# A decoder step on one core: operations of projection, samples and attention moved by a table of places, and the last norms, the tail and a first square root rearranged

## The chip, the cores and the metric

The kernel runs on one core of a Trainium2 chip. The metric is the device time of one execution in microseconds (us), the median of the runs. All engines run their own instructions in the order in which they were issued: TensorE (PE, with its weight loads as PEld), VectorE (DVE), ScalarE (ACT), GpSimd (POOL), and SP, which issues most of the transfers.

## The reference

One layer of a hybrid decoder for a prompt of 2048 rows and 8 samples of 4 rows, D = 1024, in float32:

```python
z = _rmsnorm(x, g) @ w_in                 # 1024 -> 2560: q, k, v (8 heads x 64), u, v (8 groups x 64)
for w, d in ((128, 1), (512, 4), (2048, 16)):
    s = q . k * 64**-0.5 + bias           # keys at distances 0, d, 2d, ..., w
    s = where(valid, s, NEG_INF)
    lse = logsumexp(s);  o = exp(s - lse) @ v
# the three branches are merged by position and head with weights from their softmax sums
# samples: the same with 4096 cached positions (a window of 2048 keys and values)
# the gating groups: u * (masked lower 128 x 128 W_s @ layernorm(v) + bias), in chunks of 128
x = x + concat(att, sgu) @ w_out          # output projection, 1024 x 1024
x = x + (silu(h @ w_gate) * (h @ w_up)) @ w_down    # h = _rmsnorm(x), width 2816
y = _rmsnorm(x)
```

`_rmsnorm(x, g)` is x * rsqrt(mean(x * x) + EPS) * g. Beside y, the last 2048 keys and values of prompt and samples and the normalised v rows of the samples are outputs.

## The kernel before

Every product is made in three passes: an operand is split into a high part (rounded for the fast form of float32 on PE) and a low part (the rest), and high x high, low x high and high x low are summed in PSUM. The high part is a copy on ACT, the low part a subtraction on DVE or POOL. So each weight goes through `w_load` (SP, line 231), `w_high` (ACT, line 236) and `w_low` (DVE, line 242).

The first 980 us are written as a plan. `Plan.at(step, phase, fn, *args)` notes an operation with a step, one of ten phases (early, exp, low, scores, turn, mid, values, out, misc, store) and a running number; `Plan.run` sorts by step, phase and number and calls them in that order. The order of the calls is the order of the instructions on each engine. The numbers count every call of `at` from the start of the program, so they name each operation. Steps up to 240 hold the input projection, the gating unit and the attention of the samples; from there on each of the eight heads has 20 steps.

Projection and samples. The weights run in as above; `transposed`, `value_split` (ACT, line 143, with pair as its result) and `store_values` (SP, line 379) put q, k and v into the buffers qk_d and v_d in memory; `gates`, `gated`, `gated_copy` (ACT, line 449) and `store_gated` (SP, line 452) do the gating unit, whose input v is normalised in `layer_norm_a` to `layer_norm_d` (lines 381 to 402) and split into vnh and vnl. The samples' scores are made on DVE: `key_unit` multiplies, `key_sum` (line 589) sums, `sample_bias` (lines 598 and 599) adds the bias; then `softmax_a` transposes and takes the maximum, `softmax_e` (ACT, lines 623 and 624) the exponential, `softmax_b` (DVE, lines 628 to 632) divides, `softmax_c` (PE, line 639) transposes back, and `value_high`, `value_low` (lines 663 and 667) and `value_unit` (PE, lines 678 and 679) multiply with the cached values.

Attention. A head is 16 tiles of 128 rows of the band (distances 1 and 4 together, up to five key tiles each, b0 to b15) and 4 strided steps (distance 16, four residues each, s0 to s3). A band tile goes through `band_scores` (PE, line 957), `band_bias` (DVE, line 963), `band_exp` (ACT, line 968), `band_turn` (PE transposes, line 976, and the high part ph on ACT, line 979), `low_parts` (DVE, line 998, pl), `band_values` (PE, line 1012) and `band_out`. A strided step goes through `order_queries` (POOL, line 941), `strided_scores` (PE, line 1030), `strided_bias` (DVE, lines 1035 and 1037, then a subtraction on POOL, line 1038), `strided_exp` (ACT, line 1041), `strided_sum` (DVE, line 1045), `strided_turn` (PE, line 1050; eh on ACT, line 1053; el on DVE, line 998) and `strided_values` (PE, lines 1061 and 1062). Band and strided transposes take the PSUM banks of one ring, and a bank comes free when its low part (pl or el) has been made.

At the end of a head `Stats` (POOL, line 1082, sm; PE, line 1088) and `Weights` (lines 1103 to 1135) make the factors of the branches, which are spread over the rows and written to f_d. One head later `merge_load` (SP, line 1149) brings four quarters of them back as pairs, and `merge` (POOL, lines 1160, 1162 and 1164) multiplies and adds. Meanwhile `load_head` loads the next head but one: q and k (line 901), the bias (line 906), the values for the strided steps in 8 transfers (line 917) and the values for the band in one of 1 MB (line 921). `roll` (line 173) copies a piece of the cache to the outputs.

From 980 us the rows are worked in blocks: output projection, the second norm (`norm2_half`, `norm2_gain`, `norm2_square`, `rms_b`, `norm2_scale`; lines 1497 to 1531), transposes (PE, line 1543), gate and up products (lines 1729 to 1731). At the end comes the down projection of the last rows (class `Down`): a step `n` sums and splits two operands (`split`: ACT lines 1926 and 1927, DVE lines 1928 and 1929), multiplies them for four row tiles (`mats`, lines 1943 to 1945) and adds to the rows (`evict`, line 1963). The final norm of a tile is `square` (ACT, line 1970), `mean` (DVE, lines 1990 and 1991), `root` (ACT, line 1994), `scale` (DVE, lines 150 to 154 and 2000), `scale_rest` (ACT, line 2004) and `out` (SP, line 2009). `behind(k, ...)` queues such a part k steps later. The last TAIL = 3 steps are done tile by tile, each tile with its own final norm behind it.

Of the kernel before, what the change touches and what calls it, by code (L numbers as in the profile page):

```python
# [19 lines left out]
P = 128  # L20
# [27 lines left out]

class Plan:
# [21 lines left out]
def hymba_step(ctx: ExitStack, tc: tile.TileContext, A: dict, O: dict):  # L71
# [1425 lines left out]
    def rms_b(s1, n, more=None):  # L1497
        if more is not None:
            dve.tensor_scalar(s1[:n, 0:1], s1[:n, 0:1], more[:n], None, op0=OP.add)
        dve.tensor_scalar(s1[:n, 1:2], s1[:n, 0:1], 1.0 / D, EPS, op0=OP.mult, op1=OP.add)  # L1500
        act.activation(s1[:n, 2:3], s1[:n, 1:2], AF.Sqrt)
# [6 lines left out]
    def norm2_half(B, i, junk=None):  # L1508

        B.s1[i] = s1 = fl.tile([P, 4], F32, name="s1", tag="s1", bufs=6)  # L1510
        act.activation(zn_tile() if junk is None else junk, B.acc[i][:, 0:512], AF.Square, accum_out=s1[:, 0:1])

    def norm2_gain(B, i):
        n = B.rows[i]
        B.xn[i] = square_tile() if n == P else fa.tile([P, D], F32, name="xns", tag="acc5")
        pool.tensor_mul(B.xn[i][:n], B.acc[i][:n], gain[0][:n])

    def norm2_square(B, i, junk):

        n = B.rows[i]  # L1520
        s1 = B.s1.get(i)
        if s1 is not None:
            act.activation(B.X[0][:, i, 0:512] if junk is None else junk, B.acc[i][:, 512:1024], AF.Square, accum_out=s1[:, 3:4])
            return s1, s1[:, 3:4]
        s1 = fl.tile([P, 4], F32, name="s1", tag="s1", bufs=6)
        act.activation(B.X[0][:, i, 0:D] if n == P else square_tile()[:n], B.acc[i][:n], AF.Square, accum_out=s1[:n, 0:1])
        return s1, None

    def norm2_scale(B, i, r):
        n = B.rows[i]  # L1530
        act.activation(B.xn[i][:n], B.xn[i][:n], AF.Copy, scale=r)
# [56 lines left out]
    def norm2_slot(B, k, order):  # L1588
# [278 lines left out]
    TAIL = 3  # L1867

    class Down:
# [97 lines left out]

        def square(self, i, c):
            x = self.acc[i][:, c * 512:(c + 1) * 512]
            act.activation(zn_tile(), x, AF.Square, accum_out=self.sq[i][:, (0, 3)[c == i % 2]:][:, 0:1])  # L1970

        def early_half(self, i):

            self.sq[i] = self.p2.tile([P, 4], F32, name="sq", tag="sq", bufs=8)
            c = i % 2
            x = self.acc[i][:, c * 512:(c + 1) * 512]
            self.behind(1, self.square, i, c)
            self.behind(1, pool.tensor_mul, x, x, gain[1][:, c * 512:(c + 1) * 512])

        def late_half(self, i, quick=False):  # L1980
            steps = (1, 2, 2, 3, 3, 4) if quick else (1, 2, 3, 4, 5, 6)
            for k, fn in zip(steps, (self.late_square, self.mean, self.root, self.scale, self.scale_rest, self.out)):
                self.behind(k, fn, i)
# [4 lines left out]
        def mean(self, i):  # L1988
            s1 = self.sq[i]
            dve.tensor_scalar(s1[:, 0:1], s1[:, 0:1], s1[:, 3:4], None, op0=OP.add)  # L1990
            dve.tensor_scalar(s1[:, 1:2], s1[:, 0:1], 1.0 / D, EPS, op0=OP.mult, op1=OP.add)

        def root(self, i):
            act.activation(self.sq[i][:, 2:3], self.sq[i][:, 1:2], AF.Sqrt)

        def scale(self, i):
            r = rms_c(self.sq[i], P)
            cs = slice((1 - i % 2) * 512, (2 - i % 2) * 512)
            x = self.acc[i][:, cs]
            dve.scalar_tensor_tensor(x, x, r, gain[1][:, cs], op0=OP.mult, op1=OP.mult)  # L2000

        def scale_rest(self, i):
            x = self.acc[i][:, i % 2 * 512:(i % 2 + 1) * 512]
            act.activation(x, x, AF.Copy, scale=self.sq[i][:, 2:3])
# [6 lines left out]
        def run(self):  # L2011
            self.queue = {}
            for n in range(2 * NS - TAIL):
# [13 lines left out]
                if n >= NJ and m < 4 and not (wide and j % 2):  # L2027
# [5 lines left out]
                    elif ps_ in (5, 6):  # L2033
                        self.late_half(i + ps_ - 5, not wide)
# [6 lines left out]
        def tail(self):  # L2041
            n0 = 2 * NS - TAIL
            for _ in range(4):
                tick()
            for n in sorted(self.queue):
                for fn, args in self.queue[n]:
                    fn(*args)

            def begin(m):
                i = 8 + 2 * m + 1  # L2050
                self.mean(i)
                self.root(i)

            def root_end(m):
                return rms_c(self.sq[8 + 2 * m + 1], P)

            def finish(m, r):
                i = 8 + 2 * m + 1
                x = self.acc[i]
                act.activation(x[:, 512:], x[:, 512:], AF.Copy, scale=r)  # L2060
                dve.scalar_tensor_tensor(x[:, 0:512], x[:, 0:512], r, gain[1][:, 0:512], op0=OP.mult, op1=OP.mult)
                self.out(i)

            r = {}
            for m in range(4):
                for n in range(n0, 2 * NS):
                    self.mats(n, (m,))
                if m:
                    begin(m - 1)
                    r[m - 1] = root_end(m - 1)  # L2070
                self.evict(1, 6, m, self.Y)
                self.late_square(8 + 2 * m + 1)
                if m:
                    finish(m - 1, r[m - 1])
            begin(3)
            finish(3, root_end(3))
# [156 lines left out]

    def first_block(B):
# [29 lines left out]

        def root_ahead():
            t_ = fl.tile([P, 4], F32, name="s1", tag="s1", bufs=6)
            act.activation(t_[:, 0:1], ident[:, 0:1], AF.Sqrt)
# [25 lines left out]
    def next_block(B, downs, finals):  # L2293
# [23 lines left out]
        for y in range(4):  # L2317
# [3 lines left out]
            else:  # L2321
                later(10 + 3 * y, sources, B, y // 2, y % 2 * 2, y % 2 * 2 + 1)
        for fn in downs:
# [201 lines left out]
```

## Time and profile before

| what | us |
|---|---|
| median of 3 runs | 2489.65 |
| the runs | 2488.77, 2489.65, 2495.33 |
| the profiled execution, its own time | 2492.2 |
| its span | 2490.4 |
| PE busy, share of the span | 2406.0, 97% |
| DVE, ACT and POOL busy | 1688.3, 1218.5, 1119.8 |
| mean granted TensorE clock | 0.988 |

Line numbers are those of the kernel before. A row of the timeline has start, duration, engine, line, operation, output and inputs, and in brackets the idle time before it with what ended that. A row of the waits has who waited for what, the total in us, how often, and the longest. A row of the windows has for each engine the busy time and the count of instructions, then the granted clock, the share of the transfer engines and GB/s.

### The profile page before, as it was taken

The page shows a single profiled execution, that of the slowest core. Times are in us where ns is not written, and L with a number is a line of the kernel's source. Part 1 is how long each engine was busy: PE and PEld are TensorE (multiplying, and loading weights), DVE is VectorE, ACT ScalarE, POOL GpSimd, SP SyncE. Part 2 cuts the span into 40 slices and gives each one's busy share as a digit, 9 for nine tenths or more (in the row PEclk, how much of TensorE's full clock was granted, in tenths as well). Part 3 has the DMA queues.
Part 4 walks back from the last instruction along what each step waited for, and adds up shares of the span by engine and source line. Part 5 has one row for each costly group of instructions (what it writes and reads, how often), then busy time and mean ns, then how long its engine had stood idle before and what let it go on. Part 6 is the DMA issues. An engine that isn't in the chain of part 4 may idle for free. (4 is left out here: it accounts for less than half of the span.)

```text
span 2490.4 us, 39073 instructions
## 1 busy us (share of the span) xinstructions
PE 2406.0 (97%) x13360; PEld 2128.3 (85%) x13360; DVE 1688.3 (68%) x3097; ACT 1218.5 (49%) x2414; POOL 1119.8 (45%) x859
## 2 busy tenths in 40 slices
PE   9999899999998889999999999999999999999997
PEld 6788667777888877999998899999799998888886
DVE  4378777335888786756655677766566666877886
ACT  6424344345777765433333533333465554445544
POOL 1004323013566666666664576667468883100100
PEclk9999999999999999999999999999999999999998
DMA  8863872688788856466668266676747677766842
GB/s 265 258 194 108 293 244 72 214 255 257 242 263 273 250 153 222 155 207 199 209 214 288 90 225 232 246 254 219 253 155 236 221 230 254 264 196 231 298 136 87
DMA packets 318087, 539.12 MB, mean 216 GB/s; under 512 B 28854, under 2 KB 152151, under 8 KB 312002
## 3 DMA queue, kind: packets, MB, share of 16 engines
q1 hardware_dynamic: 317536, 536.51, 65.8%
q8 instruction: 106, 1.74, 0.3%
q14 instruction: 91, 0.75, 0.1%
q10 hardware_dynamic: 354, 0.12, 0.0%
HBM read 420.38 MB, written 186.28 MB: 244 GB/s over the span
## 5 line engine op out<-in xcount | busy, mean ns | idle before, releaser
L1729 PE MATMUL ps_m<-xh,op 128*128 128x384 f32 (+5 forms) x1932 | 612.2, 317 | 0.3 <-DVE raw L1766 0.2
L1730 PE MATMUL ps_m<-xl,op 128*128 128x384 f32 (+5 forms) x1932 | 612.0, 317 | 0.0
L1731 PE MATMUL ps_m<-xh,op 128*128 128x384 f32 (+5 forms) x1932 | 611.3, 316 | 0.0
L1666 POOL TENSOR_TENSOR op<-fr,op 128x512 fp32r<-128x512 f32 x286 | 404.6, 1431 | 90.3 <-ACT op L1662 66.4
L1729 PEld LDWEIGHTS ps_m<-xh,op 128*128 128x128 f32 x1932 | 363.9, 188 | 1.6 <-DVE raw L1766 0.6
L1730 PEld LDWEIGHTS ps_m<-xl,op 128*128 128x128 f32 x1932 | 363.8, 188 | 0.6
L1731 PEld LDWEIGHTS ps_m<-xh,op 128*128 128x128 f32 x1932 | 364.2, 189 | 0.0
L1666 POOL TENSOR_TENSOR op<-pair,op 128x512 fp32r<-128x512 f32 x126 | 168.8, 1340 | 156.5 <-DVE hr L1791 86.1
L339 PE MATMUL ps_s<-wh,xh 128*128 128x512 f32 x480 | 197.8, 412 | 5.7 <-ACT xh L143 5.7
L1662 ACT ACTIVATE op<-fr 128x512 fp32r<-128x512 f32 x330 | 196.5, 621 | 10.0 <-DMA fr<-ab_d 6.2
L340 PE MATMUL ps_s<-wl,xh 128*128 128x512 f32 x480 | 190.7, 397 | 0.0
L341 PE MATMUL ps_s<-wh,xl 128*128 128x512 f32 x480 | 190.1, 396 | 0.0
L1780 ACT ACTIVATE ps_t<-zn 128x384 f32<-128x384 f32 (+2 forms) x132 | 60.0, 454 | 251.0 <-DVE zn L1759 205.7
L1926 ACT ACTIVATE op<-fr 128x512 fp32r<-128x512 f32 x140 | 88.7, 634 | 181.5 <-issue 87.7
L2036 POOL TENSOR_TENSOR ac<-ac,final_g 128x512 f32<-128x512 f32 x12 | 19.5, 1624 | 319.5 <-ACT zn L1970 311.2
L1928 DVE TENSOR_TENSOR op<-fr,op 128x512 fp32r<-128x512 f32 x140 | 102.2, 730 | 75.2 <-ACT op L1926 75.2
L1662 ACT ACTIVATE op<-pair 128x512 fp32r<-128x512 f32 x126 | 79.0, 627 | 109.9 <-DVE pair L1652 109.9
L339 PEld LDWEIGHTS ps_s<-wh,xh 128*128 128x128 f32 x480 | 92.2, 192 | 37.2 <-issue 10.3
L341 PEld LDWEIGHTS ps_s<-wh,xl 128*128 128x128 f32 x480 | 91.7, 191 | 20.6 <-DVE xl L146 0.2
L1943 PE MATMUL ps_m<-op 128*128 128x512 f32 x280 | 108.9, 389 | 0.0
L1944 PE MATMUL ps_m<-op 128*128 128x512 f32 x280 | 108.9, 389 | 0.0
L1945 PE MATMUL ps_m<-op 128*128 128x512 f32 x280 | 108.9, 389 | 0.0
(551 smaller groups left out, 5877.3 us busy)
## 6 DMA issues: line engine op xcount, KB each, us to landing
fr<-in_w_gate_dram SPq DMA_DIRECT2D x132, 256.0 KB
out_ks_dram<-in_cache_k_dram SPq DMA_DIRECT2D x56, 512.0 KB
out_vs_dram<-in_cache_v_dram SPq DMA_DIRECT2D x56, 512.0 KB
fr<-in_w_up_dram SPq DMA_DIRECT2D x110, 256.0 KB
fr<-ab_d SPq DMA_DIRECT2D x88, 256.0 KB
a<-h_d SPq DMA_DIRECT2D x80, 256.0 KB
fr<-t_d SPq DMA_DIRECT2D x80, 256.0 KB
raw<-in_w_in_dram SPq DMA_DIRECT2D x72, 256.0 KB
```

The source lines that it names most:

```text
L339: pe.matmul(o[j], xh[:, k, :], wh, start=(k == 0), stop=False)
L340: pe.matmul(o[j], xh[:, k, :], wl, start=False, stop=False)
L341: pe.matmul(o[j], xl[:, k, :], wh, start=False, stop=(k == KD - 1))
L1662: act.activation(ops[f, j][0], ab[f][j], AF.Copy)
L1666: (eng or pool).tensor_sub(lo_, ab[f][j], hi.bitcast(F32))
L1729: pe.matmul(out, wh[:, ks], xh[:, :, k], start=(k == 0), stop=False)
L1730: pe.matmul(out, wh[:, ks], xl[:, :, k], start=False, stop=False)
L1731: pe.matmul(out, wl[:, ks], xh[:, :, k], start=False, stop=(k == 3))
L1928: dve.tensor_sub(wl, w, wh.bitcast(F32))
L1943: pe.matmul(banks[m], hh[:, ts], wh, start=first, stop=False, skip_group_check=more)
L1944: pe.matmul(banks[m], hh[:, ts], wl, start=False, stop=False, skip_group_check=more)
L1945: pe.matmul(banks[m], hl[:, ts], wh, start=False, stop=j == NJ - 1, skip_group_check=more)
```

## The change

A table gives 282 of the planned operations another place, by steps and by phases. Its first lines, and how it is used:

```diff
+MOVES = {
+    0: (-1, 0), 1: (-1, 0), 2: (-1, 0), 59: (2, 0), 108: (-1, 0), 109: (-1, 0), 110: (-1, 0), 114: (2, 0),
+    115: (2, 0), 116: (2, 0), 144: (0, -2), 156: (-2, 0), 164: (0, -2), 177: (1, 0), 216: (-1, 0), 218: (1, 0),
...
     def at(self, step, phase, fn, *args):
-        self.events.append((step, self.PHASES.index(phase), self.n, fn, args))
+        steps, phases = MOVES.get(self.n, (0, 0))
+        place = max(0, min(len(self.PHASES) - 1, self.PHASES.index(phase) + phases))
+        self.events.append((step + steps, place, self.n, fn, args))
         self.n += 1
```

In the projection and the samples most moves are by one to three steps: numbers 108 to 110 and 114 to 116 are load, high and low part of the weights 44 and 46; many key sums come a step later; gates, their copies and stores 577 to 589 three steps later. In the heads the same moves come again and again: the band's second tile and its low parts by a phase, the strided sums two phases earlier, weights_e a step or a phase away, the loads of the next heads one to three steps later, one or two of the factor loads one or two steps away. In the changed kernel all line numbers of this part are 44 higher.

On SP, in the head from about 750 us, this is the stretch with the loads of the values (`v`, lines 917 and 921, 961 and 965 after) and of the factors of the head before (`pair`, line 1149, 1193 after); out_ks_dram is the roll. Before:

```order
L917 DMA v_7479<-v_d_67 16x16x128 x8
L173 DMA out_ks_dram<-in_cache_k_dram 16x8192
L921 DMA v_7542<-v_d_67 128x16x128
L1149 DMA pair_7564<-f_d_69 128x2x512
L1149 DMA pair_7566<-f_d_69 128x2x512
L173 DMA out_ks_dram<-in_cache_k_dram 16x8064
L1149 DMA pair_7729<-f_d_69 128x2x512
L173 DMA out_ks_dram<-in_cache_k_dram 16x8192
L901 DMA qh_7785<-qk_d_66 128x1x2048
```

And now:

```order
L961 DMA v_7479<-v_d_67 16x16x128 x8
L217 DMA out_ks_dram<-in_cache_k_dram 16x8192
L1193 DMA pair_7567<-f_d_69 128x2x512
L965 DMA v_7578<-v_d_67 128x16x128
L1193 DMA pair_7594<-f_d_69 128x2x512
L217 DMA out_ks_dram<-in_cache_k_dram 16x8064
L1193 DMA pair_7710<-f_d_69 128x2x512
L217 DMA out_ks_dram<-in_cache_k_dram 16x8192
L1193 DMA pair_7813<-f_d_69 128x2x512
```

The first of the pair loads stands ahead of the 1 MB load of v instead of behind it; the second and third stand one place further on.

On PE, in the same head, this is the stretch around the strided transposes (line 1050, 1094 after) of the last strided step, with those of the band (line 976, 1020 after), scores (line 957, 1001) and band products (line 1012, 1056). Before:

```order
L957 MATMUL ps_s_7761<-k_7268,qh_7238 128x256
L957 MATMUL ps_s_7761<-k_7268,ql_7295 128x256
L1050 MATMUL ps_t0_7764<-ident_80,e3_7681 128x128 x4
L976 MATMUL ps_t1_7772<-ident_80,e_7711 128x128 x4
L1012 MATMUL ps_o3_7731<-ph_7556,ve_6995 128x256
L1012 MATMUL ps_o3_7731<-pl_7557,ve_6995 128x256
```

And now:

```order
L1020 MATMUL ps_t0_7761<-ident_80,e_7725 128x128 x4
L1001 MATMUL ps_s_7767<-k_7293,qh_7241 128x256
L1001 MATMUL ps_s_7767<-k_7293,ql_7314 128x256
L1001 MATMUL ps_s_7770<-k_7293,qh_7241 128x384
L1001 MATMUL ps_s_7770<-k_7293,ql_7314 128x384
L1094 MATMUL ps_t1_7773<-ident_80,e3_7681 128x128 x4
L1056 MATMUL ps_o3_7733<-ph_7559,ve_7028 128x256
L1056 MATMUL ps_o3_7733<-pl_7560,ve_7028 128x256
```

The band's transposes of the tile e have moved from behind the strided ones of e3 to ahead of them, and the scores of a further tile (two rows with 384 columns) stand between.

On DVE, in the samples at about 280 us, this is the stretch from the maximum of a softmax (line 618, 662 after) to its division (lines 628 to 630, 672 to 674 after), with the low parts of weights wl (line 242, 286) and the samples' products and sums (lines 583 and 589, 627 and 633). Before:

```order
L618 TENSOR_SCALAR nm_2599<-nm_2599 128x1
L242 SCALAR_TENSOR_TENSOR wl_2603<-raw_2531,g1c_85,wh_2587 128x512
L589 TENSOR_REDUCE S_far_121<-pr_2553 128x8
L242 SCALAR_TENSOR_TENSOR wl_2625<-raw_2555,g1c_85,wh_2621 128x512
L589 TENSOR_REDUCE S_far_121<-pr_2580 128x8
L583 TENSOR_TENSOR pr_2636<-kv_2535,qb_2401 128x512
L242 SCALAR_TENSOR_TENSOR wl_2642<-raw_2582,g1c_85,wh_2640 128x512
L628 TENSOR_SCALAR nm_2599<-nm_2599 128x1
L629 RECIPROCAL nm_2599<-nm_2599 128x1
L630 TENSOR_SCALAR X_s_1370<-X_s_1370,nm_2599 128x900
```

And now:

```order
L662 TENSOR_SCALAR nm_2600<-nm_2600 128x1
L633 TENSOR_REDUCE S_far_121<-pr_2527 128x8
L286 SCALAR_TENSOR_TENSOR wl_2624<-raw_2553,g1c_85,wh_2620 128x512
L633 TENSOR_REDUCE S_far_121<-pr_2551 128x8
L627 TENSOR_TENSOR pr_2635<-kv_2531,qb_2396 128x512
L672 TENSOR_SCALAR nm_2600<-nm_2600 128x1
L673 RECIPROCAL nm_2600<-nm_2600 128x1
L674 TENSOR_SCALAR X_s_1370<-X_s_1370,nm_2600 128x900
L676 TENSOR_TENSOR px_2642<-X_s_1370,masks_120 128x64
```

Of the three low parts of weights between maximum and division one is left.

The rest of the change is in the norms and the tail. In the norms the sum of squares goes straight into the square root, the gain of the first slot is multiplied on DVE, and the scale is cut in two:

```diff
     def rms_b(s1, n, more=None):
         if more is not None:
-            dve.tensor_scalar(s1[:n, 0:1], s1[:n, 0:1], more[:n], None, op0=OP.add)
+            dve.tensor_scalar(s1[:n, 1:2], s1[:n, 0:1], 1.0 / D, more[:n], op0=OP.mult, op1=OP.add)
+            act.activation(s1[:n, 2:3], s1[:n, 0:1], AF.Sqrt, bias=more[:n], scale=1.0 / D)
+            return
...
-            norm2_gain(B, cur)
+            norm2_gain(B, cur, dve if k == 1 else pool)
...
-        act.activation(B.xn[i][:n], B.xn[i][:n], AF.Copy, scale=r)
+        for c in range(0, D, 512):
+            x = B.xn[i][:n, c:c + 512]
+            act.activation(x, x, AF.Copy, scale=r)
```

The first half's sum of squares is scaled and EPS is added right behind it (one more operation on DVE, off the last sum). A square root of a constant, `root_ahead`, which the first block already had, is now called in the later blocks too, at `later(9, root_ahead)`; it loads the table of the square root ahead of its use.

In the tail TAIL is 4, the parts of the final norm are always spread over six steps, the mean is one operation, and the square root is taken from the sum directly:

```diff
-    TAIL = 3
+    TAIL = 4
...
-        def late_half(self, i, quick=False):
-            steps = (1, 2, 2, 3, 3, 4) if quick else (1, 2, 3, 4, 5, 6)
-            for k, fn in zip(steps, (self.late_square, self.mean, self.root, self.scale, self.scale_rest, self.out)):
-                self.behind(k, fn, i)
+            self.behind(2, self.part, i)
+
+        def late_half(self, i):
+            for k, fn in enumerate((self.late_square, self.mean, self.root, self.scale, self.scale_rest, self.out)):
+                self.behind(k + 1, fn, i)
...
         def mean(self, i):
-            s1 = self.sq[i]
-            dve.tensor_scalar(s1[:, 0:1], s1[:, 0:1], s1[:, 3:4], None, op0=OP.add)
-            dve.tensor_scalar(s1[:, 1:2], s1[:, 0:1], 1.0 / D, EPS, op0=OP.mult, op1=OP.add)
+            dve.tensor_scalar(self.col(i, 1), self.col(i, 0), 1.0 / D, self.col(i, 3), op0=OP.mult, op1=OP.add)
...
+            self.sums(2 * NS - 1)
+            self.split(2 * NS - 1)
             for n in sorted(self.queue):
...
+            i = tile_of(3)
+            x, y, r = self.acc[i], zn_tile(), self.col(i, 2)
+            dve.tensor_mul(y, x[:, 0:512], gain[1][:, 0:512])
             begin(3)
-            finish(3, root_end(3))
+            root_end(3)
+            c = 640
+            act.activation(x[:, c:], x[:, c:], AF.Copy, scale=r)
+            dve.tensor_scalar(x[:, 512:c], x[:, 512:c], r, None, op0=OP.mult)
+            dve.tensor_scalar(x[:, 0:512], y, r, None, op0=OP.mult)
+            self.out(i)
```

So the last split of operands is issued ahead of what is left in the queue, and the last tile's gain is multiplied ahead of its root, with the scale shared between ACT (384 columns) and DVE (128 and 512).

More of the change, by code (lines that the diff above doesn't have):

```diff
@@ L2232, in second_phase, with root_ahead @@
             later(n, last_operands, *steps, ahead=True)
+    def root_ahead():
+        t_ = fl.tile([P, 4], F32, name="s1", tag="s1", bufs=6)
+        act.activation(t_[:, 0:1], ident[:, 0:1], AF.Sqrt)
     def first_block(B):
```

55 lines of the change are left out of this document (29 added, 26 removed), and 36 rows, old and new, of the table MOVES.

## The prediction

> **What bounds the kernel now.** I read first the busy times of the page, then busy time by stretches of the program, then what the TensorE waits for in each stretch, then the timeline of one head, of the sharing of the input projection and of the last 30 us. The first lines are the page's engines and three long stretches, with the last 41 us behind them (span, PE busy, PEld, DVE, ACT, POOL, granted TensorE clock, DMA).
>
> ```profile
> PE 2406.0 (97%) x13360; PEld 2128.3 (85%) x13360; DVE 1688.3 (68%) x3097; ACT 1218.5 (49%) x2414; POOL 1119.8 (45%) x859
> ...
> 50.00:600.00 550.00, 526.58 (x2419) 409.70 (x2418) 321.39 (x579) 231.71 (x403) 126.52 (x87) 0.98 0.66 208
> 600.00:980.00 380.00, 344.39 (x2311) 309.10 (x2310) 297.84 (x629) 264.30 (x604) 224.91 (x241) 0.97 0.80 244
> 980.00:2440.00 1460.00, 1453.73 (x8303) 1346.06 (x8302) 1015.20 (x1762) 665.26 (x1301) 757.77 (x520) 1.00 0.63 216
> ...
> 2450.00:2491.00 41.00, 27.45 (x106) 21.22 (x104) 26.44 (x75) 18.11 (x44) 0.00 (x0) 0.82 0.28 103
> ```
>
> PE is the bound, and the change removes none of its products. What it can win is PE's idle time: 550 − 526.6 = 23.4 us in projection and samples, 380 − 344.4 = 35.6 us in attention, 6.3 us in the 1460 us of output projection, norms and feed-forward (it is in the norms), 13.6 us at the end. Beside idle time there is the clock. These are windows of 3.4 us, with the same columns:
>
> ```profile
> 141.90:145.30 3.40, 3.40 (x31) 3.18 (x31) 1.08 (x5) 0.00 (x0) 0.00 (x0) 1.00 0.76 266
> 145.30:148.70 3.40, 3.40 (x10) 2.62 (x9) 3.40 (x9) 0.00 (x0) 0.00 (x0) 0.50 0.16 49
> ...
> 281.80:285.20 3.40, 0.00 (x0) 0.00 (x0) 2.15 (x5) 3.39 (x7) 0.00 (x0) 1.00 1.08 302
> 285.20:288.60 3.40, 0.17 (x1) 0.20 (x2) 3.30 (x5) 2.47 (x5) 3.14 (x2) 0.50 0.94 318
> ```
>
> After a window in which PE stood (0.00) the next is granted 0.50. A whole window at 0.50 costs about half of itself; I take 1.6 us. By the granted clock over the whole trace there are six such windows in attention (at 623 two, 866, 872, 886, 896) and seven in projection and samples (145, 285 two, 313, 401 two, 476), some 20 us together; two more stand in the tail.
>
> **The change part by part. Attention.** PE's waits in 600 to 1000 (total, times, longest):
>
> ```profile
> PE ps_t L976 <- DVE el L998: 8.7, 15, 1.6
> PE ps_t L1088 <- POOL sm L1082: 3.6, 5, 0.8
> PE ps_t L1050 <- ACT e L1041: 2.7, 3, 1.4
> ...
> PE ps_o L976 <- DVE el L998: 2.4, 6, 0.5
> PE ps_s L1030 <- POOL qo L941: 2.4, 4, 1.5
> ...
> PE ps_o L1050 <- ACT e L1041: 1.4, 1, 1.4
> ```
>
> They come back in each head. One head on SP, POOL, ACT and PE (start, duration, in brackets the idle time before):
>
> ```profile
> 757.54 1.13 SPq L1182 DMA_DIRECT2D cat_d<-ob  x2
> ...
> 768.11 0.53 SPq L921 DMA_DIRECT2D v<-v_d  x1
> 768.68 3.90 SPq L1149 DMA_DIRECT2D pair<-f_d  x2
> ...
> 798.30 1.13 SPq L1182 DMA_DIRECT2D cat_d<-ob  x2
> ...
> 777.65 1.29 POOL L1160 TENSOR_TENSOR ob<-ob,pair 128x512 f32<-128x512 f32 x1 [8.07 <-DMA pair<-f_d]
> ...
> 780.16 1.04 POOL L1038 TENSOR_TENSOR e<-e,st 128x512 f32<-128x512 f32 x1
> ...
> 783.50 1.29 POOL L1160 TENSOR_TENSOR ob<-ob,pair 128x512 f32<-128x512 f32 x1
> ...
> 781.23 0.63 ACT L1041 ACTIVATE e<-e 128x512 f32<-128x512 f32 x1 [1.96 <-POOL e L1038]
> ...
> 782.58 0.81 ACT L968 ACTIVATE e<-e,st 128x640 f32<-128x640 f32 x1
> ...
> 781.92 0.66 PE L1050 MATMUL ps_t<-ident,e 128*128 128x128 f32 x4 [1.02 <-ACT e L1041]
> ```
>
> The factors of the head before (f_d, L1149) are issued behind the 1 MB load of v (L921). POOL, which takes its work in order, stands 8.07 us before merge (L1160), so the subtraction of the strided scores (L1038) starts at 780.16, the exponential on ACT at 781.23, and PE waits 1.02 us. POOL then has its merges to catch up, and is late for qo and sm too. The change issues one of the two pair loads ahead of that v load; 1 MB takes about 4 us by the 244 GB/s of the stretch. That is more than the 1.02 us, so I count the waits on e (2.7 + 1.4), sm (3.6) and qo (2.4) as gone: 10.1 us. The order of the band's transposes (L976) against the strided ones changes as well, so that its second group goes into a bank that another tile's low part frees; of the 8.7 + 2.4 us waited for el I count half, 5.5. The moves of sums and low parts by a phase lie on DVE (298 of 380 us busy) and POOL (225), under PE's work; I count them at nothing. Where that cover fails, each costs its own operation, 0.7 us on PE's path. With shorter gaps I take two of the six half-clock windows back, 3.2 us. Sum for attention: −18.8 us. Bounds: all idle time and all clock, 35.6 + 6 × 1.6 = −45; on the other side +19.3 (the second rival).
>
> **Projection and samples.** PE's waits in 50 to 600, and what stands before the largest, on DVE:
>
> ```profile
> PE ps_t L639 <- DVE X_s L630: 6.8, 1, 6.8
> PE ps_t L679 <- DVE vh L667: 3.7, 3, 2.8
> ...
> PE ps_t L430 <- ACT vnh L143: 2.5, 1, 2.5
> PE ps_t L430 <- POOL vnl L146: 1.0, 1, 1.0
> ...
> 284.47 0.75 DVE L242 SCALAR_TENSOR_TENSOR wl<-raw,g1c,wh 128x512 fp32r<-128x512 f32 x1 [1.25 <-ACT wh L236]
> 285.14 0.21 DVE L628 TENSOR_SCALAR nm<-nm 128x1 f32<-128x1 f32 x1
> ```
>
> The softmax of a sample group (L628 to L630) stood behind a weight's low part (L242) that was waiting for ACT. The change moves that weight by two steps: at most the 1.25 us that it waited and its own 0.75, of the 6.8; the sums of ACT's exponential come within that time, so I take 1.2, and since PE then starts in a window at half clock, half of that, 0.6. Key sums move one step later and the normalised v of one tile comes sooner; of the 3.5 us at L430 I take 2. Loads of values and weights change places before L679: I take 1.5 of 3.7. Of the seven half-clock windows the two gaps behind these stood before three; I take two, 3.2 us. Of the rest, small gaps, 1. Sum −8.3 us; bounds −24 (all 23.4 idle) and +5 (about two new gaps the size of the 2.8 one: a moved load or product that then comes late; the SP queue there waits as often as it works).
>
> **Norms.** At the narrow last tile between blocks, ACT and PE, and PE's waits for the scaled wide rows from 980 on:
>
> ```profile
> 1794.19 1.28 ACT L1501 ACT_TABLE_LOAD   x1
> ...
> 1796.66 1.15 ACT L1531 ACTIVATE xns<-xns,s 32x1024 f32<-32x1024 f32 x1 [0.97 <-issue]
> ...
> 1797.86 0.68 PE L1543 MATMUL ps_t<-ident,xns 32*128 32x32 f32 x8 [1.41 <-ACT xns L1531]
> ...
> PE ps_t L1543 <- ACT pair L1531: 3.6, 4, 1.5
> ```
>
> A dummy square root put earlier takes the table load, 1.28 us, out of the chain, so of the 1.41 I count 1.2. The scale (L1531) is cut into halves: its 1.15 us for 1024 columns, so the first transposes start about 0.5 us sooner at the four waits, together 1.8 of 3.6. The gain multiplied on DVE instead of POOL in one slot, and the sum's addition folded into the square root, lie behind ACT's square and I give them nothing. Sum −3.0; bounds −5.0 (all) and 0 (halves add an instruction each, 0.1 us).
>
> **Tail.** ACT and PE:
>
> ```profile
> 2464.00 0.72 ACT L2004 ACTIVATE ac<-ac,sq 128x512 f32<-128x512 f32 x1 [1.72 <-DVE sq L154]
> ...
> 2468.62 0.72 ACT L2004 ACTIVATE acc<-acc,sq 128x512 f32<-128x512 f32 x1 [1.72 <-DVE sq L154]
> ...
> 2466.41 0.69 DVE L1928 TENSOR_TENSOR op<-fr,op 128x512 fp32r<-128x512 f32 x1 [1.41 <-ACT op L1926]
> ...
> 2470.41 0.69 DVE L1928 TENSOR_TENSOR op<-fr,op 128x512 fp32r<-128x512 f32 x1 [0.79 <-ACT op L1926]
> ...
> 2470.95 0.79 PE L1943 MATMUL ps_t<-op 128*128 128x512 f32 x1 [2.70 <-ACT op L1927]
> ```
>
> Here a step takes 2468.62 − 2464.00 = 4.6 us, because ACT's scale waits for DVE's root and DVE's next operand waits for ACT behind that scale. The change spreads square, mean, root and scale over six steps, so these two no longer answer each other inside one: the two idle times on DVE go, 1.41 + 0.79 = 2.2 us; three means lose an operation like L628's 0.21 above, 0.6; one more step is done tile by tile, so its operands (two of 0.69) are ready earlier, 1.4. The last tile's scale of 0.72 for 512 columns leaves a quarter of them to DVE, 0.2. Sum −4.4; bounds −2.2 and −6.
>
> The sum: 18.8 + 8.3 + 3.0 + 4.4 = 34.5 us. From the profiled run, 2492.2 (span 2490.4), that makes 2457.7. That run lay 2.55 above the median of the three, 2489.65; against the median I say 2455.
>
> A rule that speaks against the clock part: the Trainium skill, "TensorE: Matmul & The Clock Gate", section "Part 4: PE-mode transpose", says that transposes do not count as busy for the gate the way products do. No window here holds transposes alone; the nearest is the one at 141.9, above, which is full (3.40 of 3.40 us) of 31 small matmuls, and after which 0.50 is granted, so that busy time alone does not hold the clock. By that rule attention with its transposes would trip however well it is filled (the first rival).
>
> **The rivals.** (1) Clock not won back: windows follow what PE does, not whether it stands, as at 141.9. Then both 3.2 go: 34.5 − 6.4 = 28.1, 2461 against the median. (2) Slower: the second pair load. The change sends it one step later, still behind the 1 MB load; a step is (798.30 − 757.54) / 20 = 2.04 us. If it lands after POOL comes to the second merge (783.50 now), POOL stands there instead, in front of the next L1038, and PE at the next strided transpose. Moreover b14's transposes now stand ahead of the strided ones on PE, and their exponential stands behind the strided one on ACT (782.58 after 781.23), 0.65 us more. That gives (2.04 + 0.65) × 6 heads = 16.1, with two further half-clock windows 3.2, against 7.4 from norms and tail and nothing from the projection: +12, 2502. It decides from the point at which the pair lands past 783.5. Against it: in the row of now the second merge follows without any idle time, so it already had its data. (3) Deep gain: most waits of both stages go, 0.7 × (23.4 + 35.6 + 13 × 1.6) + 7.4 = 63, 2426. For it: all these gaps are under 2 us but three, and DVE, ACT and POOL have reserves. (4) The table only shifts waits, norms and tail alone: −7.4, 2482. For it: PE's waits for el come 15 + 6 times and are not led by loads.
>
> **How the numbers follow.** Forecast with (1): 0.62, in 2437 to 2470. (3): 0.14. (4): 0.14. (2): 0.10. About 0.3%, 7.5 us, is what a measurement of this kernel tells from no change. (4) lies on that line and gives half to each side: faster 0.62 + 0.14 + 0.07 = 0.83, same 0.07, slower 0.10. The range from 2427 to 2484 leaves out (2) and the half of (3) below it.
>
> **What would show it.** Right: POOL's wait for pair<-f_d falls from about 8 us a head to under 4, no wait on e L1041 or sm L1082 over 0.3 us; PE idle in 600 to 980 near 20 us; no table load before the narrow tile; in the tail no 2.7 us gap. Wrong: attention with new gaps at L976 behind ACT's L968 or at the second merge; the number of windows at 0.50 unchanged; PE idle in 50 to 600 over 23 us.

## The result and the profile after

The changed kernel takes 2469.82 us (median of four runs, 2468.77 to 2472.12) against 2489.53 for the one before: 19.7 us less, ratio 0.9918 with a 95% interval of 0.9901 to 0.9936. The forecast was 2455, 34.5 us less, with a range of 2427 to 2484. The profiled execution took 2472.12, its span 2470.3. Line numbers after are 44 higher in the planned part and 45 or more higher in the norms and the tail.

To see where the time went I cut both spans at the same four instructions: the first score of attention, its last band product, the first down product, the end. Stretches of the kernel before (length, then PE, PEld, DVE, ACT, POOL busy, granted clock, DMA):

```profile
0.00:585.60 585.60, 556.94 (x2509) 431.79 (x2510) 330.49 (x591) 252.24 (x424) 129.95 (x92) 0.98 0.68 213
585.60:929.20 343.60, 307.22 (x2178) 280.36 (x2176) 281.77 (x610) 253.75 (x591) 207.02 (x232) 0.97 0.80 240
929.20:2093.00 1163.80, 1157.38 (x6999) 1099.35 (x6998) 765.19 (x1346) 517.52 (x1026) 756.65 (x519) 1.00 0.63 213
2093.00:2490.40 397.40, 384.45 (x1681) 316.83 (x1679) 310.87 (x551) 195.01 (x373) 26.17 (x16) 0.98 0.61 212
```

The same stretches of the changed kernel:

```profile
0.00:576.20 576.20, 553.84 (x2508) 429.90 (x2509) 325.18 (x593) 252.91 (x424) 127.96 (x92) 0.99 0.69 216
576.20:916.10 339.90, 304.40 (x2178) 278.64 (x2176) 277.51 (x608) 253.62 (x591) 207.65 (x232) 0.97 0.83 243
916.10:2078.20 1162.10, 1158.35 (x6999) 1099.54 (x6998) 763.76 (x1349) 522.26 (x1045) 749.77 (x516) 1.00 0.64 213
2078.20:2470.30 392.10, 381.21 (x1681) 315.01 (x1679) 310.56 (x552) 196.03 (x373) 26.15 (x16) 0.99 0.62 214
```

The differences: projection and samples −9.4 us (forecast −8.3), attention −3.7 (−18.8), output projection, norms and feed-forward −1.7 (−3.0), down projection and tail −5.3 (−4.4); together −20.1. Three of the four came near what was counted. Attention did not: PE's idle time there went from 343.6 − 307.2 = 36.4 us to 339.9 − 304.4 = 35.5, although most of the waits that I had named are smaller or gone. PE's waits there in the changed kernel:

```profile
PE ps_t L1020 <- ACT e L1012: 7.7, 9, 1.3
PE ps_t L1020 <- DVE pl L1042: 6.0, 10, 1.4
PE ps_t L1132 <- POOL sm L1126: 4.9, 3, 2.9
PE ps_o L1020 <- DVE pl L1042: 2.2, 5, 0.6
PE ps_t L1020 <- DVE el L1042: 2.0, 6, 0.9
```

No wait on the strided exponential or on qo is among the first, and el fell from 8.7 to 2.0, as hoped. In their place stand the band's exponential (L1012, 7.7), the low parts pl (6.0 and 2.2), and sm, which did not fall (3.6 + 0.7 before by these waits, 4.9 + 0.2 now). One head shows how sm is late again, on SP, POOL and PE (a row SPq is SP's issuing of transfers):

```profile
801.94 0.44 SPq L965 DMA_DIRECT2D ve<-v_d  x1
802.59 3.58 SPq L1193 DMA_DIRECT2D pair<-f_d  x1
...
801.35 1.29 POOL L1204 TENSOR_TENSOR ob<-ob,pair 128x512 f32<-128x512 f32 x1 [3.15 <-DMA pair<-f_d]
...
812.62 1.28 POOL L1204 TENSOR_TENSOR ob<-ob,pair 128x512 f32<-128x512 f32 x1 [4.04 <-DMA pair<-f_d]
...
817.69 1.04 POOL L1082 TENSOR_TENSOR e<-e,st 128x512 f32<-128x512 f32 x1
818.68 0.63 POOL L1126 TENSOR_TENSOR sm<-st,sel_m 128x256 f32<-128x256 f32 x1
...
819.37 0.62 PE L1132 MATMUL ps_t<-sel_n,sm 128*128 128x16 f32 x4 [2.86 <-POOL sm L1126]
```

The first pair is there early (POOL waits 3.15 us instead of 8.19 in this head). The second is issued right behind the 1 MB load (L965), its issue takes SP 3.58 us, and POOL stands 4.04 us for it, until 812.62, in front of the strided subtraction and of sm. This is how the second rival of the prediction would work. It isn't so in every head of this profile: the first merge still waits 3.1 to 6.8 us in six of them, under 4 in two, and in the other heads the second waits 0.77 us at most.

In the samples the gap of 6.8 us before the softmax's transposes is nearly closed. DVE, POOL and PE in the changed kernel:

```profile
280.81 0.69 DVE L674 TENSOR_SCALAR X_s<-X_s,nm 128x900 f32<-128x900 f32 x1
...
281.35 2.35 POOL L190 TENSOR_TENSOR xl<-xr,xh 128x1024 fp32r<-128x1024 f32 x1 [3.66 <-ACT xh L187]
...
281.64 0.96 PE L683 MATMUL ps_t<-ident,X_s 128*128 128x128 f32 x7 [0.34 <-DVE X_s L674]
...
281.53 2.26 DVE L676 TENSOR_TENSOR px<-X_s,masks 128x64 f32<-128x64 f32 x1
...
283.84 0.30 PE L684 MATMUL ps_t<-ident,px 128*64 128x128 f32 x1 [1.24 <-DVE px L676]
```

What is left of it is 0.34 us and, one operation later, 1.24: the small product px (L676) behind the division now begins just behind POOL's subtraction and takes 2.26 us, where it takes 1.2 in the profile before.

At the narrow last tile the table load is gone from ACT's chain and PE doesn't wait; in the tail the last two of DVE's operands are 2.9 us apart (2446.45 to 2449.38) where they stood 4.0 apart (2466.41 to 2470.41), and PE has no wait there where the one of 2.70 us stood:

```profile
1780.36 0.20 ACT L1547 ACTIVATE s<-s 32x1 f32<-32x1 f32 x1 [0.21 <-DVE s L1546]
...
1782.36 0.95 PE L1592 MATMUL ps_t<-ident,xns 32*128 32x32 f32 x8
...
2446.45 0.68 DVE L1977 TENSOR_TENSOR op<-fr,op 128x512 fp32r<-128x512 f32 x1
...
2449.38 0.69 DVE L1977 TENSOR_TENSOR op<-fr,op 128x512 fp32r<-128x512 f32 x1
```

### The profile page after: what moved, and what is told of

It reads as the page before. It is cut to its first block, busy times and chain, and to the rows that moved or that the text cites. A ratio compares the mean times of both kernels' runs of the same rounds, so it can differ in the third digit from the quotient of the medians.

```text
span 2470.3 us, 39063 instructions
## 1 busy us (share of the span) xinstructions
PE 2397.8 (97%) x13360; PEld 2123.1 (86%) x13360; DVE 1677.0 (68%) x3102; ACT 1224.8 (50%) x2433; POOL 1111.5 (45%) x856
## 4 chain that ended last, share of the span: by engine, by line
PE 60%; DMA 5%; DVE 4%; POOL 4%; ACT 3%; issue 1%; SPq 0%; ACTq 0%; DVEq 0%; POOLq 0%
PE ps_m L1778 12%; PE ps_m L1779 12%; PE ps_m L1780 12%; PE ps_m L1992 3%; PE ps_m L1994 3%; PE ps_m L1993 3%; DMA pair<-f_d 2%; PE ps_o L1868 1%; DMA cat_d<-ob 1%; PE ps_o L1992 1%; PE ps_t L1992 1%; PE ps_o L1994 1%; PE ps_t L1994 1%; PE ps_t L1993 1%; PE ps_o L1993 1%
## 5 line engine op out<-in xcount | busy, mean ns | idle before, releaser
L383 PEld LDWEIGHTS ps_s<-wh,xh 128*128 128x128 f32 x480 | 91.9, 192 | 36.7 <-issue 9.9
```

What stands on the lines that cost most here:

```text
L383: pe.matmul(o[j], xh[:, k, :], wh, start=(k == 0), stop=False)
```

## The experiments

The runs differ from the changed kernel in the table alone. Each was timed beside the kernel before on the same chip, and is compared by its ratio to it; the chips' medians of the kernel before were 2490.4, 2491.07 and 2491.64.

**No table: norms and tail alone.**

```diff
 MOVES = {
-    0: (-1, 0), 1: (-1, 0), 2: (-1, 0), 59: (2, 0), ...
 }
```

Expected: 

> The changed kernel without the table: norms and tail alone. Between the two profiles the norms moved by 1.8 us and the tail by 5.3, so all theories expect about 7 us less than the kernel before, 2482 to 2483. If it is 15 or more below, the stages are not additive and the shares read off the traces are wrong.

Measured: 2482.04 us, ratio 0.9961 (0.9945 to 0.9977). Norms and tail are worth about 8 us by the times, 7.0 by the stretches of the first two profiles. The stages add up. Of these the norms have more than the first profile says: their stretch lasts 1160.8 us here and 1160.5 to 1161.1 in all the later profiles with the new norms, against 1162.1 in that one and 1163.8 before, so they are worth about 3.

**The first part of the table.**

```diff
 MOVES = {
     ...
     1502: (-2, 0),
-    1535: (1, 0), 1536: (1, 0), 1537: (1, 0), 1538: (1, 0), ...
 }
```

Expected: 

> Norms, tail and the part of the table for projection and samples (91 moves); attention in its old order. From the traces the projection moved by 9.4 us, so 16 to 17 us less than before, about 2473; attention should last the 343 to 344 us that it lasted before.

Measured: 2471.95 us, ratio 0.9922 (0.9905 to 0.9939); ten less than without the table. This is already the whole of the gain: the 91 moves of projection and samples, with norms and tail, stand within 0.1% of the full change. Attention alone, with its old order, lasts 344.3:

```profile
573.00:917.30 344.30, 307.40 (x2178) 282.00 (x2177) 282.64 (x608) 254.06 (x591) 207.09 (x232) 0.97 0.80 239
```

**Attention's loads alone, and attention's order alone**, each on top of the first part.

```diff
 # loads: of the numbers from 1535 on only those of begin, load, order_bias, merge_load and merge
-    1600: (0, -1), 1629: (0, -1), 1658: (0, -1), 1956: (0, -1), 1961: (0, -1), ...
 # order: all but those
-    1535: (1, 0), 1536: (1, 0), 1603: (-2, 0), 1616: (-2, 0), 1632: (-1, 0), ...
```

Expected: 

> As the run with the first part, and of attention's moves only those of loads and merges (37: begin, load, order_bias, merge_load, merge). Theory A (earlier factors give the gain, the new order of band and strided operations takes part of it back through waits on the exponential and on pl): 7 to 10 us less than the first part alone, so 5 or more below the changed kernel. Theory B (the order gives the gain, the loads nothing, since POOL still waits for the second pair): the same as the first part alone within 2 us.

> As the run with the first part, and of attention's moves all but those of loads and merges (154: turns, scores, low parts, sums, queries). Theory A: slower than the first part alone, by 2 to 6 us, with PE's waits on L1012 and pl as in the changed kernel and the waits on the strided exponential still there. Theory B: 3 to 4 us faster than the first part alone, as the changed kernel.

Measured: loads 2472.96 us, ratio 0.9921 (0.9906 to 0.9937); order 2473.5, ratio 0.9925 (0.9909 to 0.9941). Theory A falls in its size (the loads alone give nothing), Theory B falls too (the order alone gives nothing). The traces show each half taking waits away and paying them back inside the half. With the loads alone, PE's waits on the strided exponential are down to 1.0 us (4.7 + 0.6 with the first part alone) and those on qo to 1.5 (5.0), while those on sm are up from 2.0 + 0.7 to 8.2 + 4.9:

```profile
PE ps_t L1116 <- POOL sm L1110: 8.2, 4, 4.9
PE ps_o L1116 <- POOL sm L1110: 4.9, 1, 4.9
```

because POOL stands at a later merge, here 4.43 us at the third, whose pair SP issues only behind two cache copies, and sm is next but one behind it:

```profile
738.75 1.26 POOL L1188 TENSOR_TENSOR ob<-ob,pair 128x512 f32<-128x512 f32 x1 [4.43 <-DMA pair<-f_d]
739.98 1.04 POOL L1066 TENSOR_TENSOR e<-e,st 128x512 f32<-128x512 f32 x1
740.97 0.63 POOL L1110 TENSOR_TENSOR sm<-st,sel_m 128x256 f32<-128x256 f32 x1
...
741.65 1.03 PE L1116 MATMUL ps_o<-sel_n,sm 128*128 128x16 f32 x4 [4.89 <-POOL sm L1110]
```

With the order alone, el is down from 7.3 + 3.0 to 1.1 + 0.8 us, and the band's exponential and pl have come up in its place:

```profile
PE ps_t L1023 <- ACT e L1015: 11.2, 10, 2.9
PE ps_t L1023 <- DVE pl L1045: 6.2, 11, 1.4
```

One thing here Theory A did not expect: with the order alone the waits on the strided exponential fall too, to 0.9 us, and those on qo to 2.7, though POOL waits for its pairs as long as with the first part alone (47.3 us in all, 46.6). So an earlier pair is not the only thing that takes these waits away.

**The changed kernel once more**, with its table as it is.

Expected: 

> The changed kernel once more, on one chip with the next three. The first part alone stood at 18.5 us below before; this tells whether attention's moves together are worth anything beside it. Theory C (loads and order cancel each other's new waits only together): 20 us or more below before, attention 340 us in the profile. Theory D (attention's part is worth nothing, the 3.7 us in the first profile were scatter): 17 to 19 below before, attention 343 or more.

Measured: 2473.16 us, ratio 0.9921 (0.9906 to 0.9936); attention took 346.8 us in this profile, against 339.9 in the first one of the same kernel.

```profile
573.60:920.40 346.80, 306.02 (x2177) 280.25 (x2176) 276.82 (x608) 253.78 (x591) 207.65 (x232) 0.97 0.82 238
```

Theory D holds: attention's 191 moves together are worth nothing that can be measured, and the 3.7 us between the first two profiles are no more than two profiles of one kernel differ by, here 7 us. By one profile each, a difference of that size in this stage is no evidence.

**Both pairs first.** Attention's own moves are left out; the first and second factor load of six heads stand two steps earlier, ahead of the 1 MB load.

```diff
 MOVES = {
     ...
+    1603: (-2, 0), 1607: (-2, 0), 1632: (-2, 0), 1636: (-2, 0), 1661: (-2, 0), 1665: (-2, 0),
+    1690: (-2, 0), 1694: (-2, 0), 1719: (-2, 0), 1723: (-2, 0), 1748: (-2, 0), 1752: (-2, 0),
 }
```

Expected: 

> First part, and of attention's moves none; in their place both the first and the second factor load of each head two steps earlier, so that both stand ahead of the 1 MB load. Theory A2 (POOL stood at the second pair, and therefore was late for sm; that ate what the loads gave): no wait of POOL for a pair over 1 us at the second merge, PE's waits on the strided exponential, qo and sm together under 3 us, and 6 to 10 us less than the first part alone. Theory D: POOL is late for other reasons, time as the first part alone within 2 us.

Measured: 2467.9 us, ratio 0.9901 (0.9883 to 0.9919); 5.3 us below the changed kernel on the same chip. It is the lowest ratio of all, though its interval overlaps that of the changed kernel. Attention takes 339.3 us by its profile, and PE's idle time there is 36.7 us, no less than before, so what the gain comes from is not shown. PE's wait on sm, the largest but one of the stage:

```profile
PE ps_t L1112 <- POOL sm L1106: 8.0, 4, 3.1
```

and POOL at that merge:

```profile
728.56 1.29 POOL L1184 TENSOR_TENSOR ob<-ob,pair 128x512 f32<-128x512 f32 x1 [1.97 <-DMA pair<-f_d]
```

Theory A2 holds in half. The second merge no longer waits, and there is some gain. But the waits on sm (8.0 + 1.9 us), qo (3.5) and the strided exponential (1.0) are 14.4 us together, where A2 had under 3. In the head shown POOL waits at the third merge. There are two pair buffers, so the third pair can only be loaded when the first merge has read its own; and SP is held by a cache copy from 711.52 to 720.63 and issues that pair at 720.73. Which of the two sets its time no run tells apart.

**Without b5's move.**

```diff
-    1994: (0, -3), 2126: (0, -3), 2258: (0, -3), 2390: (0, -3), 2522: (0, -3), 2654: (0, -3),
```

Expected: 

> The changed kernel without one of its repeated moves: the band's sixth tile (b5) is transposed in its old phase in six heads, not three phases earlier. By the order the waits of 0.8 to 1.3 us on L1012 in each head belong to it. Theory A: 2 to 5 us faster than the changed kernel, the waits on L1012 down from 8.7 to about 3 us. Rival: the wait goes back to el, as before (about 0.55 a head), and the time is the same within 2 us.

Measured: 2473.81 us, ratio 0.9925 (0.9910 to 0.9939): no change. The largest of the waits on the band's exponential stands at the same tile as in the changed kernel (1.28 us, 1.29 there), so they did not belong to this move; I had read them wrongly off the order. ACT shows what that one waits behind, in the changed kernel:

```profile
793.51 0.60 ACT L1065 ACTIVATE ob<-ps_o 128x512 f32<-128x512 f32 x1 [1.72 <-DMA cat_d<-ob]
794.01 0.82 ACT L1012 ACTIVATE e<-e,st 128x640 f32<-128x640 f32 x1
...
794.97 0.66 PE L1020 MATMUL ps_t<-ident,e 128*128 128x128 f32 x4 [1.29 <-ACT e L1012]
```

The new head's first output (L1065) waits for a buffer that the store of the merged head still reads, and the band's exponential stands behind it. That store leaves when POOL's last merge of the head is done (784.75 and 1.29 us long; the store at 786.06). ACT waited for it in the kernel before as well (3.5 us in all, 6.3 now), so that it is later because of the moves is not shown.

**Both pairs first, with the order moves except b5's.**

```diff
+    1603: (-2, 0), 1607: (-2, 0), ...           # the twelve loads as above
-    1535: (1, 0), 1536: (1, 0), ...             # the changed kernel's own loads and merges
-    1994: (0, -3), 2126: (0, -3), ...           # b5
```

Expected: 

> The order moves of the changed kernel without b5's, and the loads of the run with both pairs first. If both costs are found rightly (A2 and A) this is the fastest, 8 to 12 us below the changed kernel, attention about 332 us. If Theory D holds, it is within 2 us of the changed kernel.

Measured: 2469.06 us, ratio 0.9905 (0.9886 to 0.9924). Four us below the changed kernel on its chip, and not below both pairs alone: the order moves add nothing here either. The eight runs with both pairs first, of these two kernels, took 2465.25 to 2470.66 us, and the ten of the changed kernel and of the one without b5's move, on the same chip, 2470.41 to 2475.19; so the gain of about 4 us is likely real.

**Third merges later**, on top of both pairs first.

```diff
+    1612: (1, 0), 1613: (1, 0), 1614: (1, 0), 1641: (1, 0), 1642: (1, 0), 1643: (1, 0), ...   # merge(h, 2), six heads
```

Expected: 

> As the run with both pairs first, and the three parts of each head's third merge one step later, so that on POOL they stand behind the strided subtraction and sm instead of ahead of them. Theory A3 (what is left of POOL's lateness is the third pair, which is loaded only when the first merge frees its buffer, and lands when POOL already stands at it): PE's wait on sm falls from 9.9 to under 3 us, no gap over 1.5 us at L1088's place, 4 to 7 us faster than with both pairs first, attention 334 us. Rival: the merges only pile up behind, the wait goes to qo or the next strided exponential, and the time is the same within 2 us.

Measured: 2469.4 us, ratio 0.9918 (0.9902 to 0.9934): no gain. A3's first half holds, the waits on sm are down to 0.8 us. But the wait has gone on to the band's exponential:

```profile
PE ps_t L1003 <- ACT e L995: 7.7, 5, 3.1
...
PE ps_o L1003 <- ACT e L995: 5.9, 3, 3.5
```

One head of it, on ACT and PE:

```profile
740.36 0.23 ACT L1137 ACTIVATE f<-f 128x32 f32<-128x32 f32 x1 [2.96 <-POOL f L1134]
...
740.97 0.82 ACT L995 ACTIVATE e<-e,st 128x640 f32<-128x640 f32 x1
...
741.93 0.66 PE L1003 MATMUL ps_t<-ident,e 128*128 128x128 f32 x4 [2.64 <-ACT e L995]
```

The next small operation of the head's weights on POOL (f) is now the late one; ACT waits 2.96 us for it, with the band's exponential behind. The rival of this run is right in kind: the work piles up behind the later merges. The wait went to f and the band's exponential, not to qo or the strided exponential as it had it.

**b14 ahead of the strided step**, on top of the later merges.

```diff
+    2068: (0, -1), 2074: (0, -1), 2200: (0, -1), 2206: (0, -1), ...   # low_parts(s3), band_turn(b14), six heads
```

Expected: 

> The run with the later merges, and of the order moves only two that come again in six heads: the band's fifteenth tile (b14) transposed ahead of the strided step, and the strided step's low part a phase earlier. My second rival priced the first at 0.65 us a head. By it: waits on L1012's exponential rise by 3 to 4 us, waits on el fall by 3 to 5 us, time within 2 us of the run with the later merges. By the prediction's own count (half of el's 11.1 us, nothing lost): 4 to 6 us faster.

Measured: 2469.21 us, ratio 0.9916 (0.9900 to 0.9931): the same as without. The waits on el fell only by 0.5 us (7.4 + 2.7 to 7.1 + 2.5), those on the exponential rose by 2.6 (7.7 + 5.9 to 10.9 + 5.3). That is the sign of the second rival's small price, less than its 0.65 us a head, and the prediction's half of el is not to be had from this move.

**The first part without the moves of two weights, and without those of gates and value split.**

```diff
-    108: (-1, 0), 109: (-1, 0), 110: (-1, 0), 114: (2, 0), 115: (2, 0), 116: (2, 0),     # weights 44 and 46
...
-    577: (3, 0), 578: (3, 0), 587: (3, 0), 588: (3, 0), 589: (3, 0), 616: (2, 0), 618: (2, 0),   # gates, value split
```

Expected: 

> The run with the first part, without the moves of the weights 44 and 46 (six numbers). The gap before the softmax's transposes was 6.8 before and 0.3 to 0.6 with the first part. Theory W (the low parts of weights on DVE in front of the division made it): the gap is 4 us or more again, 3 to 6 us slower than the first part. Theory G (ACT's waits on the gating unit's stores and the values' store made it): gap under 2 us, time as the first part within 2 us.

> The run with the first part, without the later gates, copies and stores of one group and the later value split (seven numbers, 577 to 589, 616 and 618). Theory G: the gap before the softmax's transposes is 4 us or more again, 3 to 6 us slower than the first part. Theory W: gap under 2 us, time as the first part within 2 us. If both this and the run without the weights' moves show a gap of 2 to 4 us, both matter.

Measured: without the weights 2477.4 us, ratio 0.9951 (0.9934 to 0.9968); without the gates 2478.07, ratio 0.9949 (0.9934 to 0.9964). By the ratios each costs about 7 us against the first part (0.9922), two thirds of what all 91 moves bring; the two were timed on another chip than the first part, and the intervals overlap a little (0.9934 to 0.9939). By its profile the stage lasts 575.2 us without the weights, within what it lasts with all 91 moves, and 580.0 without the gates. The gaps say it more clearly, without the weights and then without the gates:

```profile
PE ps_t L660 <- DVE X_s L651: 5.2, 1, 5.2
```

```profile
PE ps_t L659 <- DVE X_s L650: 4.5, 1, 4.5
```

Neither theory is right by itself: either group alone leaves most of the 6.8 us, both together take 5.2 of it (0.34 + 1.24 remain). The two groups work at different places. Without the gates' moves, ACT's exponential comes late (4.5 us of PE's wait), but the division on DVE is short. Without the weights' moves, DVE's division takes four times as long:

```profile
280.41 0.75 DVE L263 SCALAR_TENSOR_TENSOR wl<-raw,g1c,wh 128x512 fp32r<-128x512 f32 x1 [2.18 <-ACT wh L257]
...
281.52 2.71 DVE L651 TENSOR_SCALAR X_s<-X_s,nm 128x900 f32<-128x900 f32 x1
...
281.40 2.35 POOL L167 TENSOR_TENSOR xl<-xr,xh 128x1024 fp32r<-128x1024 f32 x1 [6.17 <-ACT xh L164]
```

## Why the prediction was right, and where it was not

The sign and three of four stages came out, and 2469.8 lies in the range; the size, 34.5 us for 19.7, is wrong by one term, attention.

- Projection and samples, 8.3 counted; 9.4 by the first profiles, 10 by the runs, and 9 to 16 by the ten profiles that have all 91 moves (570.1 to 576.2 us, against 585.6 and 586.6 with the old order). So it is near as a sum, or a little low, but wrong inside. The softmax term was 0.6 us and is 5.2. I counted only the low part that stood ahead of the division, let PE start in a half-speed window, and held ACT's exponential for fixed; the moves of the gates bring it earlier (without them PE waits 4.5 us for it through the division). And I did not see that 2.0 us of the division's 2.71 were not its own, though the profile before shows the same division in the other group of samples at 0.69:

```profile
427.87 0.69 DVE L630 TENSOR_SCALAR X_s<-X_s,nm 128x900 f32<-128x900 f32 x1
```

- The rest of that stage: the other two waits gave less than I took. At the gates 2.5 + 1.0 became 1.0 + 1.0, and a new one of 1.7 us came beside them. At the values' products (L679, 723 after) I counted 1.5 of 3.7, and 2.2 + 0.9 are left. Of windows at half speed the old order shows seven (two profiles), the ten profiles with all the moves one to five; I had counted on two fewer, 3.2 us, and that is right or low. At 141.9 I misread the row: of its 31 products 26 are small (33 rows by 8 columns) and five have 512 columns.
- Norms 3.0 counted, 1.7 by the first profile and about 3 by the later ones; the tail 4.4 counted, 5.3 by the profiles; together 7.4, and 8 by the run without a table. Right.
- Attention, 18.8 counted, nothing measured. The step that failed is "that is more than the 1.02 us, so I count the waits on e, sm and qo as gone". The waits on e and qo did get short, but that on sm did not, and others took their place. POOL has three merge operations for each of four pairs, 12 × 1.29 = 15.5 us a head, in a stretch that ends with the head's weights, and a pair that comes earlier for the first merge doesn't bring the others. In the head shown POOL waited at the second pair instead, ahead of sm; with the loads alone and with both pairs first it waited at the third; with the third merge later it was late for f. In every profile of this stage, whatever its order, PE is idle for 34 to 42 us. The 20 us that I gave as a sign for 600 to 980 did not come (380 − 344.6 = 35.4), nor did the one for sm. My second rival had the mechanism: POOL standing at the second merge. It came in one head in full, and sm there paid for it; but I had priced it as a loss of 12 us, with a chance of 0.10, and attention as a whole neither lost nor gained anything that can be measured. My fourth rival, in which the table only shifts waits, is right for attention and wrong for the projection.
- The half of el's wait, 5.5 us, did go, and more of it, but it was not to be had as time: waits on the band's exponential and on pl came instead (2.0 + 1.4 before to 7.7 + 1.0 after for L968, L1012; pl 1.2 + 0.4 to 6.0 + 2.2). That is a term counted without asking what the bank's next user waits for.
- The clock in attention, two windows: not shown. Profiles of the old order have 3 to 9 half-speed windows there, two of the changed kernel 5 and 7, so no run here tells whether they follow gaps or transposes, as the rule of the Trainium skill ("TensorE: Matmul & The Clock Gate", "Part 4: PE-mode transpose") would have it.

That the total still fell within the range owes something to its width. It takes in the fourth rival, too, in which attention and projection give nothing.

What is open: why PE's idle time in attention stays about the same in every order tried, what the 4 us of both pairs first come from, and whether any order gains more. A third pair buffer was not tried, nor another place for the cache copies, behind which the third pair is issued.

## What to carry to other kernels

Before counting a wait as gone, ask what the releasing engine does next: if it has a fixed amount of work before a fixed deadline, an earlier start can be lost again before it, as at the second and third merges here, unless its other inputs come earlier too. When a stage holds many small waits of about the same size, do not count them as gone until a run has shown where the next one stands: here most of the named ones went, and the time stayed. Look for the same operation elsewhere in the trace, too, before you take its duration for its own: the division stood there with 0.69 us and with 2.71. A change of many parts is best split by stages first: two runs of the twelve settled that nearly all of the table's gain came from a third of it.

## What the runs showed of the hardware

Whether a DVE operation begins just ahead of a POOL operation or just behind it can change its duration by 2 us. The division of 128x900 took 0.69 us when it began at 280.81, half a microsecond before POOL's subtraction at 281.35 (changed kernel), and 2.71 when it began at 281.52, 0.12 behind POOL's at 281.40 (without the weights' moves). Before, it took 2.71 as well:

```profile
285.58 2.71 DVE L630 TENSOR_SCALAR X_s<-X_s,nm 128x900 f32<-128x900 f32 x1
...
285.46 2.34 POOL L146 TENSOR_TENSOR xl<-xr,xh 128x1024 fp32r<-128x1024 f32 x1 [5.23 <-ACT xh L143]
```

DVE ends 0.5 us after POOL each time, as if it ran only then. Not every DVE operation is held so. In the changed kernel a sum of 128x512 begins 0.11 us behind the same kind of subtraction and takes 0.68:

```profile
275.30 2.40 POOL L190 TENSOR_TENSOR xl<-xr,xh 128x1024 fp32r<-128x1024 f32 x1
...
275.41 0.68 DVE L633 TENSOR_REDUCE S_far<-pr 128x8 f32<-128x512 f32 x1
```

The Trainium skill, "GPSIMD Engine Reference", section "1. Specifications", says that POOL's way into the on-chip memory is shared with VectorE, and that they get into each other's way where DVE runs in a mode with two ports or has two inputs there; the trace agrees, with 2.0 us for one operation. In which mode the division ran the trace does not show. So a move of half a microsecond on DVE was worth 2 us here; the price can be read from one profile only where the operation stands in it both ways.
